# The second products of the last expert stage in a fixed TensorE order, with their weights laid out by halves

## The chip, the cores and the metric

The kernel runs on one core of a Trainium2 chip, in one launch. The number that counts is the device time of the launch in microseconds (us), the median over several executions. A core has five engines that run their own instruction streams side by side and wait for each other by semaphores: TensorE (PE; its weight loads are shown apart as PEld), VectorE (DVE), ScalarE (ACT), GpSimd (POOL) and SyncE (SP), which here issues almost all transfers. Sixteen DMA engines move the data.

## The reference

The program computes a stack of layers; the change lies in the second of two layers of routed experts. Each of 16 experts picks its 64 tokens of 512, multiplies them by its weights, and the weighted results are added back at the places of those tokens:

```python
def moe_ec(h, router_w, w1, w3, w2):
    cap = EC_CAPACITY * T // N_EXPERTS          # 2 * 512 // 16 = 64
    ...
    gate, idx = lax.top_k(jnp.swapaxes(aff, 1, 2), cap)
    xg = h[bidx, idx]
    a = jnp.einsum('becd,edf->becf', xg, w1)
    g = jnp.einsum('becd,edf->becf', xg, w3)
    y = jnp.einsum('becf,efd->becd', jax.nn.silu(a) * g, w2)
    y = y * gate[..., None].astype(y.dtype)
    return jnp.zeros_like(h).at[bidx, idx].add(y.astype(h.dtype))
```

All three weights of an expert are 1024 x 1024 in f32. "Up products" are those with w1 and w3, "second products" those with w2. What comes behind is a second kind of block, which begins with a norm and one large projection, `w_in`.

## The kernel before

The kernel has five stages, ssd, moe0, attn, moe1 and ffn. In moe1 (`moe_last`) the experts are taken in eight pairs; the two experts of a pair stand side by side in TensorE's columns (`tile_position` 0 and 64). First all eight pairs do their up products (`moe_up`), and their results `aT` are kept. Then the second products follow by halves of the 1024 output features: all eight pairs for features 0 to 511, and again for features 512 to 1023. One pair in one half is called a unit here; there are 16, numbered 0 to 15. In a unit (`moe_down` with `half` set):

- the product: 16 matmuls `py<-...,aT` (L1348), eight steps k of the contraction for each of two experts. Its weights are four tiles of 1 MB from the ring (below).
- ACT scales the product by the gate into `yhi` (L1354), DVE makes the remainder `ylo` (L1355), so that hi plus lo carry f32 through the faster format.
- the slots matmul `sp` (L1361) and DVE's compare `ohT` (L1365): a 0/1 matrix that says which token each row belongs to.
- the scatter: for each of four feature tiles j, two matmuls `sc` (hi L1372, lo L1373), and DVE adds the result into the residual stream `xT` (L1374).

`sc` and `sp` take their PSUM tiles under tag "x", which the table in `Banks` sends to name D, two banks; `py` lies in name A.

The ring (`Ring`, L106 to 133) hands out weight tiles in turn: two from the pool `wm` (one transfer of 1 MB each), then three made of two `raw` buffers each (two transfers of 512 KB); there are six raw buffers, and other loads use them too. A transfer waits on SP until its buffer is free, and SP issues in order. A new ring is made for each half.

Behind the first half, `hd.feed(k)` for k = 0 to 3 starts the norm of the next block on the four finished feature tiles of `xT` (DVE and ACT write `stk`, the normed input, and sums of squares; POOL adds some). `hd.begin` then computes, tile by tile, the first four contraction steps of 12 tiles of `w_in`: each of these head tiles is 12 matmuls (`mm<-stk,hwh/hwl`, L475 to L477), with weights split into `hwh` by ACT (L176) and `hwl` by POOL (L177). Six of the 12 are handed out between the units of the second half, the other six come behind it. The later steps (k = 4 to 7, `mm<-stk,whi`) need the second half's features.

The order in which each engine sees this is made by a scheduler that weighs which instruction could go next; only inside `manual_schedule` does an engine take them in the order of the program. On the stretch of the change no such block stands before.

Of the kernel before, what the change touches and what calls it, by code (L numbers as in the profile page):

```python
# [379 lines left out]
class Kern:  # L380
# [835 lines left out]
    def moe_last(self, st, R, head):  # L1216
# [19 lines left out]
        for pr in range(8):  # L1236
            after = self.after(R[0], pr, pp)
            if pr < 8 - DEFER:
                self.moe_down(layer, pr, R, ring, ep, pp, self.moe_up(layer, pr, R, ring, ep, pp, after))
            else:  # L1240
                acts.append(self.moe_up(layer, pr, R, ring, ep, pp, after, ap))
# [81 lines left out]

    def moe_down(self, layer, pr, R, ring, ep, pp, acts, half=None):

        nc = self.nc
        big, small = R[0], (R[1] if len(R) > 1 else None)
        sel, iop = self.mk["sel"], self.mk["iop"]
        aT, cT = acts

        def bank(nm, tag, bufs):
            return pp.tile([P, 512], F32, name=nm, tag=tag, bufs=bufs)

        yb = lambda k, e: aT[:, k, 64 * e:64 * e + 64]
        ys = (lambda k, e: cT[:, k % 4, 64 * e + 32 * (k // 4):64 * e + 32 * (k // 4) + 32]) if small else None
        if half is None:
            py = [bank("py", "a", 2) for _ in range(2)]
            cy = bank("cy", "c", 2) if small else None
            self.moe_product(layer, "moe_w2", pr, ring, yb, ys, py, cy)
        else:  # L1340
            py = [None, None]
            py[half] = bank("py", "a", 2)
            for q in range(2):
                w = [ring.tile(self.I["moe_w2"][layer, 2 * pr + e, q * 512:(q + 1) * 512, half * 512:(half + 1) * 512], 4) for e in range(2)]
                for a in range(4):
                    k = 4 * q + a
                    for e in range(2):
                        nc.tensor.matmul(py[half][64 * e:64 * e + 64, :], yb(k, e), w[e][a], start=(k == 0), stop=(k == KT - 1), tile_position=(0, 64 * e))  # L1348


        def scaled(src, gate):
            hi = ep.tile([P, 512], F32R, name="yhi", tag="yhi", bufs=2)
            lo = ep.tile([P, 512], F32R, name="ylo", tag="ylo", bufs=2)
            nc.scalar.activation(hi, src, AF.Copy, scale=gate)  # L1354
            nc.vector.scalar_tensor_tensor(lo, src, gate, hi.bitcast(F32), op0=ALU.mult, op1=ALU.subtract)  # L1355
            return hi, lo

        def slots(s, cols):
            n = s.n
            ps = bank("sp", "x", 2)  # L1360
            nc.tensor.matmul(ps[:, 0:n], sel[:, pr].rearrange("p e j -> p (e j)"), s.slotT, start=True, stop=True)  # L1361
            r = []
            for cix in cols:
                t = ep.tile([P, 512], F32R, name="ohT", tag="ohT", bufs=2)
                nc.vector.tensor_scalar(t[:, 0:n], ps[:, 0:n], iop[:, cix:cix + 1], None, op0=ALU.is_equal)  # L1365
                r.append(t[:, 0:n])
            return r

        def scatter(s, y, o, k, kk):
            n, c, res = s.n, s.c, s.res  # L1370
            ps = bank("sc", "x", 2)
            nc.tensor.matmul(ps[:, 0:n], y[0][:, kk * P:(kk + 1) * P], o, start=True, stop=False)  # L1372
            nc.tensor.matmul(ps[:, 0:n], y[1][:, kk * P:(kk + 1) * P], o, start=False, stop=True)  # L1373
            nc.vector.scalar_tensor_tensor(res[:, k, :], ps[:, 0:n], self.mod(layer, 5, c, k), res[:, k, :], op0=ALU.mult, op1=ALU.add)  # L1374

        ob = slots(big, (0,))[0]
        for hf in (range(2) if half is None else (half,)):
            y = scaled(py[hf], big.gate[:, pr:pr + 1])
            for j in range(4):
                scatter(big, y, ob, hf * 4 + j, j)  # L1380
        if small:
            y = scaled(cy, small.gate[:, pr:pr + 1])
            for hf, o in enumerate(slots(small, (1, 2))):
                for j in range(4):
# [1096 lines left out]
```

## Time and profile before

| | us |
|---|---|
| median of 3 executions | 3331.31 (3325.92 to 3332.93) |
| the profiled execution | 3335.19 |
| its span in the trace | 3333.5 |
| product 0 of the stage scaled (yhi starts) | 2230.05 |
| product 7, the last of the first half | 2312.68 |
| product 8, the first of the second half | 2329.70 |
| product 15, the last | 2424.3 |
| first late matmul of the next block | 2447.55 |

The times of instructions count from the span's start and come from one profiled execution. In a timeline row the first number is the start, the second the length, and what stands in brackets is the engine's idle time before it and what ended it. Several instructions of one kind in a row are one line with a count. In the second half the trace shows each `py` matmul as records of its own, and a few records can be missing. The share of busy time over the whole span says little about this stretch, since the stages have different limits; the windows show it alone.

### The profile page before, as it was taken

To read this page: it belongs to the slowest core of one execution; us is meant where nothing else is said; L and a number is where in the kernel's file an instruction comes from. 1 tells how busy PE (TensorE), PEld (TensorE's weight loads), DVE (VectorE), ACT (ScalarE), POOL (GpSimd) and SP (SyncE) were. 2 spreads that over 40 slices of the span, in tenths; PEclk is the share of its full clock that TensorE was granted. 3 is DMA by queue.
4 is the path that set the end of the run, shared out by engine and by line. 5 is a ranking of instruction groups with operands and counts; after the bars stand their busy time and mean duration, and the time that the engine had idled before them with its cause. 6 is when DMAs were issued, how large, how long until landed. Compare 5 with 4: busy or idle time off the path is not lost.

```text
span 3333.5 us, 47840 instructions
## 1 busy us (share of the span) xinstructions
PE 3143.5 (94%) x18944; PEld 2061.6 (62%) x18944; DVE 1644.7 (49%) x3014; ACT 1165.3 (35%) x2063; POOL 963.3 (29%) x694
## 2 busy tenths in 40 slices
PE   7999999889999999999999899988999999999998
PEld 4677777777744343435757644422467778988886
DVE  5588888987521121114466410014369864763312
ACT  4344444455511111114566410001155353673222
POOL 1344555544200000002501200000054443145543
PEclk9999999999999999999999899999999999999999
DMA  7355433354388989893261599999932224443332
GB/s 251 120 168 162 143 89 93 99 168 161 124 314 318 369 323 365 322 370 131 65 215 39 215 368 409 409 389 332 339 119 75 76 69 144 134 159 105 95 92 85
DMA packets 254096, 668.60 MB, mean 201 GB/s; under 512 B 19312, under 2 KB 73456, under 8 KB 252848
## 3 DMA queue, kind: packets, MB, share of 16 engines
q1 hardware_dynamic: 243920, 645.42, 54.1%
q10 hardware_dynamic: 9952, 20.12, 1.8%
q8 instruction: 149, 2.44, 0.3%
q14 instruction: 75, 0.61, 0.1%
HBM read 651.65 MB, written 13.83 MB: 200 GB/s over the span
## 4 chain that ended last, share of the span: by engine, by line
PE 60%; DVE 9%; DMA 4%; ACT 2%; issue 2%; POOL 1%; SPq 0%; DVEq 0%; ACTq 0%; POOLq 0%
PE mm L475 6%; PE mm L477 6%; PE mm L476 6%; PE py L1348 4%; PE py L1102 3%; PE pg L1102 3%; PE pa L1102 3%; PE pa L1270 3%; DMA wm<-in_moe_w_dram 3%; PE pg L1270 2%; PE gth L343 2%; PE cy L1104 2%; PE cg L1104 2%; PE ca L1104 2%; PE pv L1564 1%
## 5 line engine op out<-in xcount | busy, mean ns | idle before, releaser
L446 POOL TENSOR_TENSOR wlo<-raw,whi 128x1024 fp32r<-128x1024 f32 (+3 forms) x207 | 460.8, 2228 | 639.1 <-ACT whi L445 605.6
L445 ACT CAST whi<-raw 128x1024 fp32r<-128x1024 f32 (+2 forms) x291 | 285.9, 984 | 478.0 <-PE mm L476 204.9
L475 PE MATMUL mm<-stk,whi 128*128 128x512 f32 (+2 forms) x944 | 342.8, 363 | 0.3 <-DVE pt__23886 L1709 0.3
L477 PE MATMUL mm<-stk,wlo 128*128 128x512 f32 (+2 forms) x944 | 336.2, 356 | 0.0
L476 PE MATMUL mm<-stk,whi 128*128 128x512 f32 (+2 forms) x944 | 335.0, 355 | 0.0
L475 PE MATMUL pin<-hhi,whi 128*128 128x256 f32 (+1 forms) x768 | 272.2, 355 | 5.3 <-DVE acc L813 3.8
L477 PE MATMUL pin<-hhi,wlo 128*128 128x256 f32 (+1 forms) x768 | 266.3, 347 | 0.0
L476 PE MATMUL pin<-hlo,whi 128*128 128x256 f32 (+1 forms) x768 | 263.9, 344 | 0.0
L475 PEld LDWEIGHTS mm<-stk,whi 128*128 128x128 f32 (+1 forms) x944 | 179.9, 191 | 33.3 <-issue 7.9
L58 POOL TENSOR_TENSOR sqa<-sqa,sq 128x256 f32<-128x256 f32 (+1 forms) x56 | 64.6, 1154 | 467.7 <-DVE acc L204 409.9
L476 PEld LDWEIGHTS mm<-stk,whi 128*128 128x128 f32 (+1 forms) x944 | 179.8, 190 | 30.1 <-issue 6.1
L1166 POOL TENSOR_TENSOR cT<-cT,scc 128x256 f32<-128x256 f32 x56 | 39.6, 736 | 545.4 <-ACT scc L1165 544.9
L477 PEld LDWEIGHTS mm<-stk,wlo 128*128 128x128 f32 (+1 forms) x944 | 179.2, 190 | 25.9 <-issue 1.1
L475 PEld LDWEIGHTS pin<-hhi,whi 128*128 128x128 f32 x768 | 147.0, 192 | 46.9 <-issue 20.9
L1188 DVE TENSOR_TENSOR ac<-ac,pg 128x512 f32<-128x512 f32 x16 | 11.0, 687 | 301.3 <-PE pg L1102 301.3
L476 PEld LDWEIGHTS pin<-hlo,whi 128*128 128x128 f32 x768 | 147.2, 192 | 19.9 <-DVE hlo L602 2.7
L477 PEld LDWEIGHTS pin<-hhi,wlo 128*128 128x128 f32 x768 | 147.1, 192 | 18.5 <-issue 1.7
L813 DVE SCALAR_TENSOR_TENSOR acc<-pin,cwh,acc 128x511 f32<-128x511 f32 (+3 forms) x256 | 148.5, 607 | 15.1 <-ACT acc L808 13.5
L1302 DVE TENSOR_TENSOR ac<-ac,pg 128x512 f32<-128x512 f32 x16 | 11.0, 685 | 249.7 <-PE pg L1270 249.7
L867 DVE SCALAR_TENSOR_TENSOR m<-ab,acum,m 128x128 f32<-128x128 f32 x192 | 121.3, 675 | 22.1 <-POOL m L865 22.1
L446 DVE TENSOR_TENSOR wlo<-raw,whi 128x1024 fp32r<-128x1024 f32 (+1 forms) x84 | 105.4, 1258 | 40.6 <-ACT whi L445 37.0
L872 POOL TENSOR_TENSOR ce<-ce,xc 128x1024 f32<-128x1024 f32 (+1 forms) x48 | 103.4, 2155 | 39.6 <-ACT ce L871 39.5
(716 smaller groups left out, 7179.3 us busy)
## 6 DMA issues: line engine op xcount, KB each, us to landing
wm<-in_moe_w_dram SPq DMA_DIRECT2D x255, 1024.0 KB, 9.5
raw<-in_moe_w_dram SPq DMA_DIRECT2D x258, 512.0 KB, 9.0
raw<-in_ada_w_dram SPq DMA_DIRECT2D x96, 512.0 KB, 4.7
raw<-in_w_f_dram SPq DMA_DIRECT2D x68, 512.0 KB, 3.7
raw<-in_w_ssd_in_dram SPq DMA_DIRECT2D x48, 512.0 KB, 4.5
ab<-aS SPq DMA_DIRECT2D x96, 256.0 KB, 4.7
raw<-in_w_in_dram SPq DMA_DIRECT2D x33, 512.0 KB, 3.7
raw<-in_w_ssd_out_dram SPq DMA_DIRECT2D x32, 512.0 KB, 3.8
```

The source lines that it names most:

```text
L445: nc.scalar.copy(hi[:, 0:n], raw[:, 0:n])
L446: (eng or self.lo).tensor_tensor(lo[:, 0:n], raw[:, 0:n], hi[:, 0:n].bitcast(F32), op=ALU.subtract)
L475: nc.tensor.matmul(ps, wh, ah, start=start, stop=False)
L476: nc.tensor.matmul(ps, wh, al, start=False, stop=False)
L477: nc.tensor.matmul(ps, wl, ah, start=False, stop=stop)
L813: nc.vector.scalar_tensor_tensor(o, p_[:, lo + s:hi + s], tap(j), o, op0=ALU.mult, op1=ALU.add)
L867: nc.vector.scalar_tensor_tensor(m[:, r, :], ab[:, r, :], acum[:, c, 4 * g + r:4 * g + r + 1], m[:, r, :], op0=ALU.subtract, op1=ALU.min)
L872: nc.gpsimd.tensor_tensor(ce[:, j0:j1, :], ce[:, j0:j1, :], conv["C"][:, o:o + P].unsqueeze(1).to_broadcast([P, j1 - j0, P]), op=ALU.mult)
L1102: nc.tensor.matmul(pb[z][o:o + 32, :], lb(k, e)[:, 32 * h:32 * h + 32], w[e][k % 2][:, z * 512:(z + 1) * 512], tile_position=(0, o), **f)
L1104: nc.tensor.matmul(pc[o:o + 32, :], ls(k, e), w[e][k % 2][:, h * 512:(h + 1) * 512], tile_position=(0, o), **f)
L1270: nc.tensor.matmul(pb[hf][64 * e:64 * e + 64, :], lb(k, e), w[e][a][:, hf * 512:(hf + 1) * 512], tile_position=(0, 64 * e), **f)
L1348: nc.tensor.matmul(py[half][64 * e:64 * e + 64, :], yb(k, e), w[e][a], start=(k == 0), stop=(k == KT - 1), tile_position=(0, 64 * e))
```

## The change

The second products get a function of their own, `moe_halves`, and `moe_down` goes. Four things differ:

- PE's order is that of the program: product of unit u, scatter of unit u-1, slots of the next unit, and from unit 9 on one head tile. Seven head tiles stand in front of the last scatter, five behind it.
- the scatter outputs take tags "x" and "c" in turn, so names D and B with two banks each; the slots matmul stays on D.
- one ring runs over all 16 units.
- w2 of the second layer is laid out on the host as [half, expert, partition, step k, 512]. A partition of a wm tile is then one run of 8 KB and that of a raw buffer one of 4 KB, with 16 KB from one partition to the next; before it was four, or two, runs of 2 KB.

```diff
-        v = src.rearrange("(a p) n -> p a n", p=P)
+        v = src if len(src.shape) == 3 else src.rearrange("(a p) n -> p a n", p=P)
...
-        for hf in range(2):
-            ring = Ring(self, self.wm1[:1], 3)
-            for i in range(DEFER):
-                self.moe_down(layer, 8 - DEFER + i, R, ring, ep, pp, acts[i], hf)
-                for _ in range(HEAD * (i + 1) // (2 * DEFER) - HEAD * i // (2 * DEFER)):
...
+        self.moe_halves(layer, R[0], ep, pp, acts, hd)
+        return hd
+
+    def moe_halves(self, layer, big, ep, pp, acts, hd):
...
+        ring = Ring(self, self.wm1[:1], 3)
...
+        def product(pr, half):
+            py, aT = bank("py", "a"), acts[pr][0]
+            for q in range(2):
+                w = [ring.tile(self.I["moe_w2h"][half, 2 * pr + e, :, 4 * q:4 * q + 4, :], 4) for e in range(2)]
...
+        def scatter(y, o, half):
+            for j in range(4):
+                k = 4 * half + j
+                ps = bank("sc", "xc"[j % 2])
+                for z in range(2):
+                    nc.tensor.matmul(ps, y[z][:, j * P:(j + 1) * P], o, start=(z == 0), stop=(z == 1))
+                nc.vector.scalar_tensor_tensor(big.res[:, k, :], ps, self.mod(layer, 5, 0, k), big.res[:, k, :], op0=ALU.mult, op1=ALU.add)
+
         fill = iter(())
+        with self.tc.manual_schedule(engines={mybir.EngineType.PE}):
+            last, o = None, slots(0)
+            for u in range(16):
+                half, pr = divmod(u, 8)
+                y = product(pr, half)
+                if last:
+                    scatter(*last)
+                last = (y, o, half)
+                if u < 15:
+                    o = slots((u + 1) % 8)
+                if u == 8:
+                    for k in range(4):
+                        hd.feed(k)
+                    fill = hd.begin(ep, pp)
+                elif u > 8:
+                    next(fill, None)
+            scatter(*last)
         for _ in fill:
             pass
...
+    A["moe_w2h"] = i["moe_w2"][1].reshape(NE, KT, P, 2, 512).transpose(3, 0, 2, 1, 4)
```

Outside moe1's second products the order of instructions is the same on every engine. Where it moves, on PE in the first half, before (`py` product, `sc` scatter outputs, `sp` slots):

```order
L1372 MATMUL sc<-ohT,yhi 128x512 x2
L1373 MATMUL sc<-ohT,ylo 128x512 x2
L1372 MATMUL sc<-ohT,yhi 128x512
L1373 MATMUL sc<-ohT,ylo 128x512
L1348 MATMUL py<-raw,aT 64x512 x2
L1372 MATMUL sc<-ohT,yhi 128x512
L1373 MATMUL sc<-ohT,ylo 128x512
L1348 MATMUL py<-raw,aT 64x512 x5
L1361 LDWEIGHTS sel
L1361 MATMUL sp<-xslotT,sel 128x512
```

and now:

```order
L1266 MATMUL py<-raw,aT 64x512 x8
L1266 MATMUL py<-wm,aT 64x512 x8
L1279 MATMUL sc<-ohT,yhi 128x512
L1279 MATMUL sc<-ohT,ylo 128x512
L1279 MATMUL sc<-ohT,yhi 128x512
L1279 MATMUL sc<-ohT,ylo 128x512
L1279 MATMUL sc<-ohT,yhi 128x512
L1279 MATMUL sc<-ohT,ylo 128x512
L1279 MATMUL sc<-ohT,yhi 128x512
L1279 MATMUL sc<-ohT,ylo 128x512
L1254 LDWEIGHTS sel
L1254 MATMUL sp<-xslotT,sel 128x512
```

Before, the scatter of a unit began right behind its product, and part of it stood inside the next product; now the scatter behind a product is that of the unit before, with hi and lo of one output together, and the slots matmul behind it.

On PE in the second half (`mm<-stk,hwh` and `hwl` are the head tiles), before:

```order
L475 MATMUL mm<-stk,hwh 128x512
L1372 MATMUL sc<-ohT,yhi 128x512 x2
L476 MATMUL mm<-stk,hwh 128x512
L1373 MATMUL sc<-ohT,ylo 128x512 x2
L477 MATMUL mm<-stk,hwl 128x512
L475 MATMUL mm<-stk,hwh 128x512
L476 MATMUL mm<-stk,hwh 128x512
L477 MATMUL mm<-stk,hwl 128x512
L1372 MATMUL sc<-ohT,yhi 128x512
L1373 MATMUL sc<-ohT,ylo 128x512
L475 MATMUL mm<-stk,hwh 128x512
```

and now, one head tile (nine of its twelve matmuls are between the two pieces):

```order
L1279 MATMUL sc<-ohT,yhi 128x512
L1279 MATMUL sc<-ohT,ylo 128x512
L1254 LDWEIGHTS sel
L1254 MATMUL sp<-xslotT,sel 128x512
L475 MATMUL mm<-stk,hwh 128x512
L476 MATMUL mm<-stk,hwh 128x512
L477 MATMUL mm<-stk,hwl 128x512
L1266 MATMUL py<-wm,aT 64x512 x8
L1266 MATMUL py<-raw,aT 64x512 x8
L1279 MATMUL sc<-ohT,yhi 128x512
```

Before, head matmuls and scatter matmuls mixed; now a whole head tile stands between slots and the next product.

On DVE where the first half ends (`xT<-sc` scatter adds, `stk` and `acc` the feeds, `ohT` the compare behind the slots matmul), before:

```order
L1374 SCALAR_TENSOR_TENSOR xT<-sc,mods_81,xT 128x512 x4
L199 SCALAR_TENSOR_TENSOR stk<-xT,gg,stk 128x512
L204 TENSOR_SCALAR acc_18078<-sqa,fin_18050 128x512
L199 SCALAR_TENSOR_TENSOR stk<-xT,gg,stk 128x512
L206 SCALAR_TENSOR_TENSOR acc_18078<-sq,fin_18050,acc_18078 128x512
L199 SCALAR_TENSOR_TENSOR stk<-xT,gg,stk 128x512
L206 SCALAR_TENSOR_TENSOR acc_18078<-sq,fin_18050,acc_18078 128x512
L1365 TENSOR_SCALAR ohT<-sp,iop 128x512
L1355 SCALAR_TENSOR_TENSOR ylo<-py,xgate,yhi 128x512
L1374 SCALAR_TENSOR_TENSOR xT<-sc,mods_81,xT 128x512 x4
```

and now:

```order
L1271 SCALAR_TENSOR_TENSOR ylo<-py,xgate,yhi 128x512
L1280 SCALAR_TENSOR_TENSOR xT<-sc,mods_81,xT 128x512 x3
L1256 TENSOR_SCALAR ohT<-sp,iop 128x512
L199 SCALAR_TENSOR_TENSOR stk<-xT,gg,stk 128x512
L204 TENSOR_SCALAR acc_18078<-sqa,fin_18050 128x512
L199 SCALAR_TENSOR_TENSOR stk<-xT,gg,stk 128x512
L206 SCALAR_TENSOR_TENSOR acc_18078<-sq,fin_18050,acc_18078 128x512
L199 SCALAR_TENSOR_TENSOR stk<-xT,gg,stk 128x512
L206 SCALAR_TENSOR_TENSOR acc_18078<-sq,fin_18050,acc_18078 128x512
L1280 SCALAR_TENSOR_TENSOR xT<-sc,mods_81,xT 128x512
L1271 SCALAR_TENSOR_TENSOR ylo<-py,xgate,yhi 128x512
L1280 SCALAR_TENSOR_TENSOR xT<-sc,mods_81,xT 128x512 x3
```

In both, the feeds stand in one piece. Before, they followed the last adds of the first half and stood in front of `ohT` of unit 8; now `ohT` of unit 9 is in front of them, and the first add of unit 8's scatter behind them.

## Rows read from the trace of the kernel before

**Rows 1.** The page: span, and busy time of PE.

```profile
span 3333.5 us, 47840 instructions
...
PE 3143.5 (94%) x18944; PEld 2061.6 (62%) x18944; DVE 1644.7 (49%) x3014; ACT 1165.3 (35%) x2063; POOL 963.3 (29%) x694
```

**Rows 2.** Busy time by windows: first half, switch, second half, tail.

```profile
core 0: us, PE busy (x) PEld busy (x) DVE busy (x) ACT busy (x) POOL busy (x), PEclk, DMA share, GB/s
2230.00:2312.68 82.68, 74.51 (x287) 24.05 (x285) 30.33 (x42) 4.81 (x7) 0.00 (x0) 1.00 0.97 355
2312.68:2329.70 17.02, 14.29 (x43) 4.12 (x43) 12.30 (x14) 5.44 (x9) 4.75 (x3) 0.80 0.77 275
2329.70:2424.30 94.60, 91.36 (x358) 38.33 (x359) 30.30 (x42) 12.89 (x22) 10.10 (x8) 1.00 0.92 331
2424.30:2447.55 23.25, 20.70 (x80) 15.98 (x81) 17.79 (x15) 13.38 (x22) 13.64 (x12) 0.93 0.54 195
```

**Rows 3.** DMA totals: 2060 to 2200 (up products), then 2235 to 2252.

```profile
DMA packets 15057, 57.26 MB, mean 409 GB/s; under 512 B 1094, under 2 KB 1094, under 8 KB 15051
...
DMA packets 3375, 6.57 MB, mean 386 GB/s; under 512 B 171, under 2 KB 171, under 8 KB 3374
```

**Rows 4.** ACT's scaling line L1354: instances, and what ended its idle time.

```profile
L1354 ACT ACTIVATE yhi<-py,xgate x16: 687/687/689, 2230.0 to 2424.3; 128x512 fp32r<-128x512 f32 x16
...
  PE py L1348: 126.5, 16
```

**Rows 5.** Timeline of PE, one unit of the first half (start, length, engine, line).

```profile
2291.72 0.50 PE L1372 MATMUL sc<-ohT,yhi 128*128 128x512 f32 x1 [0.61 <-DVE xT L1374]
...
2293.29 0.37 PE L1361 MATMUL sp<-xslotT,sel 16*128 16x512 bf16 x1 [0.18 <-DVE xT L1374]
2293.60 0.64 PE L1348 MATMUL py<-wm,aT 128*64 128x512 f32 x1
...
2295.36 0.59 PE L1348 MATMUL py<-wm,aT 128*64 128x512 f32 x1
...
2295.79 0.59 PE L1348 MATMUL py<-wm,aT 128*64 128x512 f32 x1
...
2301.45 0.73 PE L1372 MATMUL sc<-ohT,yhi 128*128 128x512 f32 x2 [0.77 <-ACT yhi L1354]
```

**Rows 6.** Timeline at the half switch, PE's, then SP's.

```profile
2317.84 1.84 PE L1348 MATMUL py<-wm,aT 128*64 128x512 f32 x2 [0.34 <-DMA wm<-in_moe_w_dram]
2320.45 5.35 PE L1348 MATMUL py<-wm,aT 128*64 128x512 f32 x13 [0.78 <-DMA wm<-in_moe_w_dram]
...
2312.63 0.92 SPq L125 DMA_DIRECT2D wm<-in_moe_w_dram  x2
```

**Rows 7.** Timeline of PE in the second half, scatter and head matmuls.

```profile
2344.01 0.39 PE L1372 MATMUL sc<-ohT,yhi 128*128 128x512 f32 x1
2344.24 0.40 PE L1373 MATMUL sc<-ohT,ylo 128*128 128x512 f32 x1
2344.47 0.40 PE L475 MATMUL mm<-stk,hwh 128*128 128x512 f32 x1
```

**Rows 8.** Timeline of DVE at the half switch: adds, feeds, ohT.

```profile
2316.32 1.41 DVE L1374 SCALAR_TENSOR_TENSOR xT<-sc,mods,xT 128x512 f32<-128x512 f32 x2 [0.17 <-PE sc L1373]
2317.66 0.74 DVE L199 SCALAR_TENSOR_TENSOR stk<-xT,gg,stk 128x512 fp32r<-128x512 f32 x1
...
2319.37 1.75 DVE L206 SCALAR_TENSOR_TENSOR acc<-sq,fin,acc 128x512 f32<-128x512 f32 x1
...
2325.72 0.74 DVE L1365 TENSOR_SCALAR ohT<-sp,iop 128x512 fp32r<-128x512 f32 x1
```

**Rows 9.** Timeline of PE in the tail, up to the first late matmul.

```profile
2435.70 0.50 PE L477 MATMUL mm<-stk,hwl 128*128 128x512 f32 x1 [0.55 <-POOL hwl L177]
...
2440.77 0.77 PE L477 MATMUL mm<-stk,hwl 128*128 128x512 f32 x1 [2.00 <-POOL hwl L177]
...
2447.55 0.39 PE L475 MATMUL mm<-stk,whi 128*128 128x512 f32 x1
```

More of the change, by code (lines that the diff above doesn't have):

```diff
@@ L1224, in moe_last @@
         sx = ExitStack()
-        ring = Ring(self, self.wm1[:-1], 3, [(self.pool(sx, "moe_wx", bufs=DEFER // 2), DEFER // 2)])
+        ring = Ring(self, self.wm1[:-1], 3, [(self.pool(sx, "moe_wx", bufs=4), 4)])
         place = []
@@ L1236, in moe_last @@
         for pr in range(8):
[L1237 to L1241, printed above, removed]
+            acts.append(self.moe_up(layer, pr, R, ring, ep, pp, self.after(R[0], pr, pp), ap))
         wa.close()
@@ L1244, in moe_last, with slots @@
         hd = head()
-        fill = iter(())
-        for hf in range(2):
-            ring = Ring(self, self.wm1[:1], 3)
-            for i in range(DEFER):
-                self.moe_down(layer, 8 - DEFER + i, R, ring, ep, pp, acts[i], hf)
-                for _ in range(HEAD * (i + 1) // (2 * DEFER) - HEAD * i // (2 * DEFER)):
+        self.moe_halves(layer, R[0], ep, pp, acts, hd)
+        return hd
+    def moe_halves(self, layer, big, ep, pp, acts, hd):
+        nc = self.nc
+        sel, iop = self.mk["sel"], self.mk["iop"]
+        ring = Ring(self, self.wm1[:1], 3)
+        bank = lambda nm, tag: pp.tile([P, 512], F32, name=nm, tag=tag, bufs=2)
+        def slots(pr):
+            ps = bank("sp", "x")
+            nc.tensor.matmul(ps, sel[:, pr].rearrange("p e j -> p (e j)"), big.slotT, start=True, stop=True)
+            t = ep.tile([P, 512], F32R, name="ohT", tag="ohT", bufs=2)
+            nc.vector.tensor_scalar(t, ps, iop[:, 0:1], None, op0=ALU.is_equal)
+            return t
+        def product(pr, half):
+            py, aT = bank("py", "a"), acts[pr][0]
+            for q in range(2):
+                w = [ring.tile(self.I["moe_w2h"][half, 2 * pr + e, :, 4 * q:4 * q + 4, :], 4) for e in range(2)]
+                for a in range(4):
+                    k = 4 * q + a
+                    for e in range(2):
+                        nc.tensor.matmul(py[64 * e:64 * e + 64, :], aT[:, k, 64 * e:64 * e + 64], w[e][a], start=(k == 0), stop=(k == KT - 1), tile_position=(0, 64 * e))
+            hi = ep.tile([P, 512], F32R, name="yhi", tag="yhi", bufs=2)
+            lo = ep.tile([P, 512], F32R, name="ylo", tag="ylo", bufs=2)
+            gate = big.gate[:, pr:pr + 1]
+            nc.scalar.activation(hi, py, AF.Copy, scale=gate)
+            nc.vector.scalar_tensor_tensor(lo, py, gate, hi.bitcast(F32), op0=ALU.mult, op1=ALU.subtract)
+            return hi, lo
+        def scatter(y, o, half):
[5 more added lines that the diff above has]
+                nc.vector.scalar_tensor_tensor(big.res[:, k, :], ps, self.mod(layer, 5, 0, k), big.res[:, k, :], op0=ALU.mult, op1=ALU.add)
+        fill = iter(())
+        with self.tc.manual_schedule(engines={mybir.EngineType.PE}):
[13 more added lines that the diff above has]
+                elif u > 8:
@@ L1322, in moe_up @@
         return aT, cT
[L1324 to L1384, printed above, removed]
-                    scatter(small, y, o, hf * 4 + j, j)
@@ L2315 @@
 APART = 3
-DEFER = 8
 STAGES = ["ssd", "moe0", "attn", "moe1", "ffn"]
@@ L2440, in prepare @@
     A["w_ao"] = wtiles(w)
-    for n in ("moe_w1", "moe_w3", "moe_w2"):
+    for n in ("moe_w1", "moe_w3"):
         A[n] = i[n]
+    A["moe_w2"] = i["moe_w2"][0:1]
+    A["moe_w2h"] = i["moe_w2"][1].reshape(NE, KT, P, 2, 512).transpose(3, 0, 2, 1, 4)
     w = i["w_in_2"][0]
```

7 lines of the change are left out of this document (1 added, 6 removed).

## The prediction

> **What bounds the kernel now.** I read the page first: TensorE (PE) is busy for 94% of the span [rows 1], so only a place where PE waits, or where its work itself shrinks, can give time. The change touches one stretch, the second products of the last expert stage, from the first scaling of a product (yhi at 2230.05) to the first late matmul of the block behind it (2447.55). The table of windows cuts this stretch into first half, switch, second half and tail [rows 2]. In it PE works 74.51 of 82.68 us, then 14.29 of 17.02, 91.36 of 94.60, and 20.70 of 23.25: 16.7 us without work, and 217.55 us in all. A unit (one pair of experts, one half of the features) brings 4.19 MB of weights. The spacing of the first eight units is 82.68/7 = 11.81 us, in which 355 GB/s arrive.
>
> Next, who waits. ScalarE (ACT) scales each product and is idle for 126.5 us over 16 times "until PE py" [rows 4], so ACT is no limit; PE in turn waits for ACT. The timeline of one unit shows the round [rows 5]: product, 0.77 us idle until yhi is there, two scatter outputs, 0.61 us until VectorE (DVE) has emptied a bank (the xT add), 0.18 us more in front of the slots matmul. That is a chain of PE, ACT and DVE, one after the other. The product itself starts a matmul every 0.43 us (2295.36 to 2295.79): 16 x 0.4275 = 6.84 us.
>
> Is the DMA a limit beside it? With 4 KB runs of weights (the up products before, 2060 to 2200) the queue carries 409 GB/s; with the 2 KB runs of the second products, at their start where it is filled, 386 [rows 3]. At these rates a unit takes 10.25 and 10.86 us. So the chain (11.81) stands little above the transfers, and once it is gone the transfers decide.
>
> **The change part by part.** *One unit behind.* PE's order is now product(u), scatter(u-1), slots(u+1). yhi and ylo of a unit have a whole product in which to be made, so the 0.77 goes. Scatter outputs lie alternately in D and B, four banks, so outputs 3 and 4 don't wait for adds 1 and 2, and the 0.61 goes. Without waits a scatter matmul follows the last in 0.233 us [rows 7]: 8 x 0.233 = 1.87. With the slots matmul (0.31, [rows 5]) PE needs 6.84 + 1.87 + 0.31 = 9.0 us for a unit of the first half, below 10.25: the first half becomes bound by the weights.
>
> *Layout.* The loads become 8 KB (wm) and 4 KB (raw) of one run per partition instead of 2 KB. No row here shows 8 KB weights, so the nearest rows bound it: 386 (no effect) to 409 (as the 4 KB runs). I take 409, the row with runs of the kind that the raw loads will have. Lower than 386 is rival 3.
>
> *One ring over both halves.* Before, the second half makes a new ring, whose first two loads go into the buffers used last: SyncE (SP) issues them at 2312.63, after product 7, and PE waits 0.34 and 0.78 us for them while the granted clock is 0.80 over the switch [rows 2, 6]. Now tile i is issued when tile i-5 is free, without a break at unit 8. When a pair of tiles starts to be used, three more (3.1 MB, 7.7 us of transfer) are still to come, and the pair frees its buffers within 3.4 us, so the queue does not run dry.
>
> Sum of the first half: product 0 ended at 2230.05 - 0.6 (its yhi starts some 0.6 behind the last matmul's start). Its 4.19 MB at 409 instead of 386 come 0.6 us sooner, but part of them is loaded earlier; I put its end at 2229.4. Units 1 to 8 at 10.25 give 82.0: product 8 ends at 2311.4, where it ended shortly before 2329.70. Gain so far 18 us.
>
> *Unit 9 and the feeds.* Behind scatter(7) the stage gives four feeds to DVE (stk and acc), which in the trace took from 2317.66 to 2325.72, 8.06 us, with single instructions drawn out to 1.75 where GpSimd (POOL) worked beside them [rows 8]. In the new DVE order they stand before the xT add of scatter(8). From the end of product 8 (T8) DVE has add, ylo, three adds and ohT (0.65 + some 4.1 at 0.67 to 0.75 each, ready at T8 + 4.8), the feeds (to 12.9), and the add of scatter(8) output 0 (to 13.6). The slots matmul of unit 10 reuses that bank. PE gets there at T8 + 10.25 + 1.87 = 12.1, and waits until about 13.8: 1.7 us. This is an added wait; queued behind it on PE are the first head tile and product(10), and all that follows waits too. Bounds: 0 (feeds without POOL beside them, 5.6) to 4.5 (2.9, and 1.6 for a lowered clock behind it as in the tail, (1 - 0.93) x 23.25 [rows 2]). I take 1.7. Then slots 0.31, head tile 12 x 0.233 = 2.79, product 6.84: product 10 ends at T8 + 13.8 + 9.94 + 0.3 = T8 + 24.0 = 2335.4.
>
> *Units 11 to 15.* PE now does a head tile in every unit (seven of the twelve, before six): 6.84 + 1.87 + 0.31 + 2.79 + 0.3 for the changes between kinds (before, PE was busy 91.36 for 8 x 9.02 + 6 x 2.79 = 88.9) = 12.1. The transfers need 10.25 and 0.64 for half a pair of head weights: 10.9, below 12.1, so PE decides. Five units: 60.5, product 15 ends at 2395.9. Before, it ended at about 2424.3: gain 28. The second half before shows what this rests on: 94.60 us with 91.36 of work, 11.83 a unit with six tiles in it; here seven tiles over seven units cost more a unit, and fewer are left for the tail. Head weights share six raw buffers with the ring, so a ring load six places on waits until POOL has made both hwl. In the new ACT and POOL order these casts come early enough (before yhi(9) and yhi(13), behind yhi(11), with more than 5 us to spare). I cost it at nothing; if that cover went, 2 to 3 us in each of three places.
>
> *Tail.* scatter(14) 1.87, tile seven 2.79, scatter(15) 1.87, five tiles 13.95, 0.4 between: 20.9, to 2416.8. In the tail before, PE waited 0.55 and 2.00 for hwl from POOL, and the granted clock over the tail was 0.93, which costs (1 - 0.93) x 23.25 = 1.6 [rows 2, 9]. POOL still has the same instructions in almost the same order, so I keep 4 us of these 4.2 (bounds 0 to 6): the first late matmul at 2420.8, against 2447.55. DVE's last feeds (8 to 11 us) lie beside the five tiles as before.
>
> Sum: 2447.55 - 2420.8 = 26.75 us. What follows is the same on every engine, and PE waits for nothing at 2447.55, so I carry it to the end in full. The profiled execution took 3335.19: 3308.4. The median is 3.88 below that execution: 3304.6, so 3305.
>
> **A rule against the layout.** The trace has 386 GB/s with 2 KB runs and 409 with 4 KB runs [rows 3]. The Trainium skill ("DMA: Bandwidth & Descriptors", Specifications) says that transfers of 512 B or more already go at line rate; by that rule the layout gives nothing, which is rival 1. The same table puts the HBM limit of a core near 358 GB/s; by that a unit would take 11.7 us, an estimate from that page, and about 12 us of the gain would go. The 409 of this trace speaks against the second figure here, and the step from 386 to 409 against the first.
>
> **Rivals.** *1. The rate stays at 386.* The two rates differ in more than the run length (the up products have more buffers in flight). Then units 0 to 9 take 0.61 us more each, 6 us: gain 20.7, 3311. For it: the rows don't separate the two causes. Against: the 386 stands where the DMA share is full, too. 14%.
>
> *2. The fixed order makes PE wait at every head tile.* Before, PE's order let sc and head matmuls mix; now PE stands at a tile until its hwl is there, with a product behind it. If each of the seven tiles in the loop cost what the worst one in the tail cost, 2.0 + 1.6, that is 25 us: gain 2, 3330. Against: in the loop POOL does nothing but hwl, 1.3 us each, and the weights come a unit ahead. 12%.
>
> *3. Slower: the weights land more slowly than before.* Partitions now step by 16 KB in HBM, and each transfer is 128 such runs. If the rate fell under 193.2/15 = 12.9 us a unit, that is 326 GB/s, the transfers would be the bound of all 16 units, and the kernel slower. At 300 GB/s, 14.0 us: 15 x 14.0 + 24.9 from 2229.4 ends at 2464, 17 us later, 3348. For it: no row has this step. Against: every full queue in [rows 3] runs at 386 or more. 5%.
>
> *The change doesn't do what it says*, so that PE would still wait for yhi: the order on PE excludes it.
>
> **How the numbers follow.** My forecast has 69%: 3305, on its own 3296 to 3314 (the wait at unit 10 by 1.7 less or 2.8 more, the tail by 4 less or 2 more, the rate between the two rows). Rival 1 lies inside; the range goes to 3293 and 3323, and leaves out most of rivals 2 and 3 and a little below: about 2 in 10. A difference under 0.2% (6.7 us) can't be told from none. Faster by more: forecast, rival 1 and a quarter of rival 2, 86%; within: over half of rival 2, 7%; slower: rival 3 and the rest, 7%.
>
> **What would show it.** Right: yhi every 10.2 to 10.4 us in the first half with 400 GB/s or more; no wait for a wm load and full clock around unit 8; a wait of PE for xT in front of one slots matmul, 1 to 3 us; 12.1 us a unit behind it; sc never waiting for yhi; the late matmul 27 us sooner. Wrong: yhi at 10.9 (rival 1), PE idle until hwl or a DMA at the head tiles (rival 2), or units of 13 us with the DMA full (rival 3).

## The result: 0.5% faster, within the range, by two thirds of the predicted gain

| | before | changed |
|---|---|---|
| median, us | 3330.67 (4 runs, 3325.92 to 3332.93) | 3312.69 (4 runs, 3311.26 to 3315.73) |
| the profiled execution, us | 3335.19 | 3311.26 |
| its span in the trace, us | 3333.5 | 3309.5 |

The ratio is 0.9950, with a 95% interval of 0.9937 to 0.9964: 18.0 us of the median, where 26.75 were predicted. Measured once more, beside two other kernels, the changed kernel had 3308.92 against 3325.87, a ratio of 0.9946 (0.9929 to 0.9963).

The two profiled executions differ by 24 us, and not all of that is the change. The first yhi of the stage came at 2223.71 instead of 2230.05, and 4.2 of these 6.3 us stand already at the first scaled product of the first expert layer (1008.9 against 1013.1), which is the same in both. In the eleven runs of the experiments below the start of the stage lies anywhere between 2216.5 and 2228.4. So I compare the stretch from the first yhi to the first late matmul, which holds all that the change moves. It took 217.50 us before [rows 2, 9] and 200.84 after: 16.7 us. A second profile of the changed kernel gave 199.77, so differences of a microsecond in it mean nothing.

The page of the changed kernel, the busy times of [rows 1]:

```profile
PE 3129.0 (95%) x18944; PEld 2070.5 (63%) x18944; DVE 1638.5 (50%) x3014; ACT 1165.6 (35%) x2063; POOL 965.6 (29%) x694
```

The windows of the changed kernel: product 0 to 8, 8 to 10, 10 to 15, each from yhi to yhi, and the tail; the last row is a piece of the second, which is used below.

```profile
core 0: us, PE busy (x) PEld busy (x) DVE busy (x) ACT busy (x) POOL busy (x), PEclk, DMA share, GB/s
2223.71:2307.62 83.91, 79.55 (x321) 32.11 (x320) 29.71 (x44) 5.51 (x8) 0.00 (x0) 1.00 1.02 409
2307.62:2335.68 28.06, 23.92 (x95) 11.05 (x96) 18.13 (x20) 7.76 (x13) 8.15 (x5) 0.88 0.79 299
2335.68:2401.09 65.41, 63.99 (x266) 30.76 (x267) 20.21 (x30) 9.36 (x16) 5.07 (x4) 1.00 0.86 328
2401.09:2424.55 23.46, 21.48 (x89) 16.18 (x89) 17.93 (x19) 13.51 (x23) 15.73 (x13) 1.00 0.65 235
2323.20:2328.00 4.80, 4.80 (x12) 3.40 (x12) 3.21 (x5) 0.00 (x0) 0.00 (x0) 0.52 1.02 416
```

Against [rows 2]: the first half runs with a full queue at 409 GB/s, at the full clock into unit 8 and beyond; the switch has gone as a stretch of its own. But the second window has 4.1 us without work and a clock of 0.88, and the third has 1.4 us without work. What PE waited for in the whole stretch (us in total, times, longest), before:

```profile
PE sc L1372 <- ACT yhi L1354: 7.7, 10, 0.8
PE sc L1372 <- DVE xT L1374: 3.7, 6, 0.6
```

and now:

```profile
PE py L1266 <- DMA wm<-in_moe_w2h_dram: 4.8, 4, 1.8
PE sp L1254 <- DVE xT L1280: 4.1, 1, 4.1
PE mm L477 <- POOL hwl L177: 1.7, 2, 1.1
PE py L1266 <- DMA raw<-in_moe_w2h_dram: 0.8, 1, 0.8
```

No wait for yhi is left, and none of a scatter for an add. The wait for xT stands in one place, and it is the longest of all:

```profile
2318.63 0.40 PE L1279 MATMUL sc<-ohT,ylo 128*128 128x512 f32 x1
2323.17 0.58 PE L1254 MATMUL sp<-xslotT,sel 16*128 16x512 bf16 x1 [4.14 <-DVE xT L1280]
...
2324.27 0.63 PE L476 MATMUL mm<-stk,hwh 128*128 128x512 f32 x1
2324.70 0.63 PE L477 MATMUL mm<-stk,hwl 128*128 128x512 f32 x1
```

The scatter of unit 8 ends, the slots matmul of unit 10 stands for 4.14 us, and the head tile behind it runs with matmuls 0.43 apart instead of 0.23, until 2327.7. From 2323.2 to 2328 the granted clock is 0.52 (the last of the windows above), the lower level of 1.2 instead of 2.4 GHz; ahead of the idle stretch it was 1.00. What slots waited for on DVE:

```profile
2312.24 0.74 DVE L199 SCALAR_TENSOR_TENSOR stk<-xT,gg,stk 128x512 fp32r<-128x512 f32 x1
...
2313.96 1.77 DVE L206 SCALAR_TENSOR_TENSOR acc<-sq,fin,acc 128x512 f32<-128x512 f32 x1
...
2320.71 1.74 DVE L206 SCALAR_TENSOR_TENSOR acc<-sq,fin,acc 128x512 f32<-128x512 f32 x1
2322.38 0.74 DVE L1280 SCALAR_TENSOR_TENSOR xT<-sc,mods,xT 128x512 f32<-128x512 f32 x1
```

And what worked beside it on POOL:

```profile
2313.60 4.97 POOL L58 TENSOR_TENSOR sqa<-sqa,sq 128x512 f32<-128x512 f32 x3 [408.47 <-PE py L1266]
2318.53 3.38 POOL L177 TENSOR_TENSOR hwl<-raw,hwh 128x512 fp32r<-128x512 f32 x2
```

The reader should see here that the feeds took 10.1 us (2312.24 to 2322.38) and not the 8.06 of [rows 8]: five of the eight instructions are drawn out to 1.74 to 1.78, three beside POOL's three sqa adds, as before, and two more beside two hwl.

The pace of the units, by the start of yhi (units 7 to 14 here):

```profile
2297.49 0.69 ACT L1270 ACTIVATE yhi<-py,xgate 128x512 fp32r<-128x512 f32 x1 [11.50 <-PE py L1266]
2307.62 0.69 ACT L1270 ACTIVATE yhi<-py,xgate 128x512 fp32r<-128x512 f32 x1 [9.44 <-PE py L1266]
...
2317.39 0.68 ACT L1270 ACTIVATE yhi<-py,xgate 128x512 fp32r<-128x512 f32 x1
...
2335.68 0.69 ACT L1270 ACTIVATE yhi<-py,xgate 128x512 fp32r<-128x512 f32 x1 [6.47 <-PE py L1266]
...
2348.05 0.69 ACT L1270 ACTIVATE yhi<-py,xgate 128x512 fp32r<-128x512 f32 x1 [4.28 <-PE py L1266]
...
2362.07 0.69 ACT L1270 ACTIVATE yhi<-py,xgate 128x512 fp32r<-128x512 f32 x1 [8.14 <-PE py L1266]
...
2374.49 0.69 ACT L1270 ACTIVATE yhi<-py,xgate 128x512 fp32r<-128x512 f32 x1 [1.13 <-PE py L1266]
...
2388.68 0.69 ACT L1270 ACTIVATE yhi<-py,xgate 128x512 fp32r<-128x512 f32 x1 [8.28 <-PE py L1266]
```

The first half has eight units in 83.9 us (10.49 each). From unit 10 on units of 12.4 alternate with units of 14.0 and 14.2.

Waits are the smaller part of what went. The whole stretch, before and now, and one unit without a wait in each (unit 3 before, unit 4 now), columns as above:

```profile
2230.05:2447.55 217.50, 200.81 (x766) 82.47 (x766) 90.72 (x113) 36.52 (x59) 28.49 (x22) 0.98 0.89 321
2223.71:2424.55 200.84, 188.93 (x768) 90.09 (x767) 85.98 (x113) 36.14 (x59) 28.95 (x22) 0.98 0.89 347
...
2253.87:2265.27 11.40, 11.32 (x43) 3.23 (x41) 4.41 (x6) 0.69 (x2) 0.00 (x0) 1.00 1.04 380
2255.75:2265.16 9.41, 9.41 (x42) 3.76 (x43) 4.04 (x6) 0.69 (x1) 0.00 (x0) 1.00 1.00 389
```

PE's time without work fell from 16.7 to 11.9 us, its busy time from 200.8 to 188.9 at the same mean clock. So 11.9 of the 16.7 us are the same matmuls standing closer together: before, the scatter of a unit stood in pieces inside the next product, and such a unit took 11.4 us with PE at work throughout, where 9.4 do now. e9 below puts 5 us of this on the order alone; what the rest comes from wasn't taken apart.

### The profile page after: what moved, and what is told of

Its sections match the earlier page's. It is cut to its first block, busy times and chain, and to the rows that moved or that the text cites. A ratio compares the mean times of both kernels' runs of the same rounds, so it can differ in the third digit from the quotient of the medians.

```text
span 3309.5 us, 47859 instructions
## 1 busy us (share of the span) xinstructions
PE 3129.0 (95%) x18944; PEld 2070.5 (63%) x18944; DVE 1638.5 (50%) x3014; ACT 1165.6 (35%) x2063; POOL 965.6 (29%) x694
## 4 chain that ended last, share of the span: by engine, by line
PE 60%; DVE 8%; DMA 5%; ACT 2%; issue 2%; POOL 1%; SPq 0%; DVEq 0%; ACTq 0%; POOLq 0%
PE mm L475 7%; PE mm L476 7%; PE mm L477 7%; PE py L1102 3%; PE pg L1102 3%; PE pa L1102 3%; PE pa L1313 3%; PE py L1266 3%; PE pg L1313 2%; DMA wm<-in_moe_w_dram 2%; PE gth L343 2%; PE cy L1104 2%; PE cg L1104 2%; PE ca L1104 2%; DMA raw<-in_moe_w_dram 1%
## 5 line engine op out<-in xcount | busy, mean ns | idle before, releaser
L445 ACT CAST whi<-raw 128x1024 fp32r<-128x1024 f32 (+2 forms) x291 | 285.7, 984 | 477.7 <-PE mm L476 200.8
```

What stands on the lines that cost most here:

```text
L445: nc.scalar.copy(hi[:, 0:n], raw[:, 0:n])
```

## The experiments

All stretches are from the first yhi to the first late matmul, in us, of one profile for each kernel (the second profile of the changed kernel, e10, is 1.1 us shorter than the first, so a cost read against it is that much larger and a saving that much smaller); the columns behind it are its parts from yhi to yhi. Medians stand beside runs of the kernel before on the same chip, shared by the kernels that were measured together (e1 to e4, e5 to e8, e9 to e11).

| kernel | median | before beside it | ratio (95%) | stretch | units 0 to 8 | 8 to 10 | 10 to 15 | tail |
|---|---|---|---|---|---|---|---|---|
| before (profile) | | | | 217.5 | 99.6 | 27.8 | 66.8 | 23.3 |
| changed | 3312.69 | 3330.67 | 0.9950 (0.9937 to 0.9964) | 200.8 | 83.9 | 28.1 | 65.4 | 23.5 |
| e1 old layout | 3318.26 | 3326.60 | 0.9967 (0.9955 to 0.9980) | 206.4 | 88.1 | 27.5 | 67.3 | 23.5 |
| e2 before, new layout | 3328.79 | 3326.60 | 1.0001 (0.9989 to 1.0013) | 216.6 | 98.8 | 27.8 | 66.8 | 23.3 |
| e3 ring per half | 3314.22 | 3326.60 | 0.9966 (0.9954 to 0.9979) | 207.2 | 89.5 | 29.0 | 64.3 | 24.4 |
| e4 slots on C | 3307.37 | 3326.60 | 0.9934 (0.9918 to 0.9951) | 195.1 | 84.3 | 22.9 | 64.5 | 23.5 |
| e5 scatter on D only | 3320.67 | 3325.65 | 0.9990 (0.9981 to 1.0000) | 213.7 | 88.9 | 30.8 | 69.4 | 24.6 |
| e6 scatter at once | 3319.57 | 3325.65 | 0.9977 (0.9968 to 0.9986) | 210.0 | 88.0 | 27.9 | 70.4 | 23.8 |
| e7 head weights apart | 3308.98 | 3325.65 | 0.9943 (0.9928 to 0.9958) | 197.5 | 84.4 | 27.9 | 61.8 | 23.5 |
| e8 e4 and e7 together | 3298.39 | 3325.65 | 0.9918 (0.9905 to 0.9931) | 191.5 | 83.7 | 22.4 | 61.9 | 23.5 |
| e9 scheduler's order | 3311.12 | 3325.87 | 0.9951 (0.9936 to 0.9966) | 203.7 | 86.9 | 25.6 | 67.3 | 23.9 |
| e10 changed, again | 3308.92 | 3325.87 | 0.9946 (0.9929 to 0.9963) | 199.8 | 84.8 | 27.6 | 64.0 | 23.4 |
| e11 e8, again | 3301.46 | 3325.87 | 0.9922 (0.9902 to 0.9942) | 192.1 | 84.4 | 22.4 | 61.9 | 23.4 |

**e1, the old layout of the weights in the changed kernel.**

```diff
-                w = [ring.tile(self.I["moe_w2h"][half, 2 * pr + e, :, 4 * q:4 * q + 4, :], 4) for e in range(2)]
+                w = [ring.tile(self.I["moe_w2"][1, 2 * pr + e, q * 512:(q + 1) * 512, half * 512:(half + 1) * 512], 4) for e in range(2)]
...
```

> The changed kernel with w2 as it lay before, in runs of 2 KB. Measured from the first yhi to the first late matmul (before 217.5 us, changed kernel 200.8). Theory, the run length sets the rate of the full queue: the first half falls from 409 to about 386 GB/s, its eight units take 86 to 88 us instead of 83.9, and the second half waits some more for loads; the stretch is 204 to 208 us, so 3 to 7 us of the 17 come from the layout. Rival, the rate comes from the queue being kept full and not from the runs: 400 GB/s or more and the stretch within 1.5 us of 200.8.

Its first half, busy times and rate as in the windows above:

```profile
2225.52:2313.62 88.10, 81.31 (x321) 30.55 (x321) 29.71 (x44) 5.51 (x9) 0.00 (x0) 1.00 1.05 385
```

385 GB/s with a DMA share of 1.05, against 409 with 1.02 (400 with 1.01 in the second profile, e10): same kernel, same ring, only the layout differs. The theory holds, with 88.1 for 86 to 88 predicted and a stretch of 206.4. The layout is worth 5.5 us. The edit changes the steps between the runs along with their length, so it doesn't part the two; for the length speaks that the up products, whose weights lie as before in runs of 4 KB, have 409 as well [rows 3]. The Trainium skill ("DMA: Bandwidth & Descriptors", Specifications) would have 2 KB at line rate like anything from 512 B; the 385 and 409 here say that for this load it is not.

**e2, the layout alone, in the kernel before.** The line of e1 the other way round, in `moe_down`, with the weights laid out to match.

> The kernel before with the new layout of w2 alone. Theory, its first half is bound by the chain product, yhi, scatter, add (11.8 us a unit) and not by the weights: first half 82 to 83 us as before (82.6), the stretch 214 to 218, and the same time within 0.1%. Rival, the weights bind already there: first half 78 us or less and the kernel 5 us or more faster.

The stretch is 216.6, the ratio 1.0001: nothing. Up to unit 6 the units take the same 11.4 to 12.2 us as before; units 7 and 8 together take 28.1 instead of 29.0. Together with e1 this says that the layout pays only once the old order has gone: the same edit is worth nothing before the rest of the change and 5.5 us after it.

**e3, a new ring for the second half.**

```diff
-        ring = Ring(self, self.wm1[:1], 3)
+        rings = [Ring(self, self.wm1[:1], 3)]
...
         def product(pr, half):
+            if half == 1 and pr == 0:
+                rings.append(Ring(self, self.wm1[:1], 3))
+            ring = rings[-1]
             py, aT = bank("py", "a"), acts[pr][0]
```

> The changed kernel with a new ring for the second half, as before the change. Theory: the first loads of unit 8 wait for product 7, PE waits for them and its clock is lowered, the stretch grows by 4 to 8 us to 205 to 209. Rival, scatter and slots cover the loads: within 1.5 us of 200.8.

```profile
2304.82 1.04 PE L1269 MATMUL py<-wm,aT 128*64 128x512 f32 x2 [2.04 <-DMA wm<-in_moe_w2h_dram]
2307.20 4.92 PE L1269 MATMUL py<-wm,aT 128*64 128x512 f32 x13 [1.34 <-DMA wm<-in_moe_w2h_dram]
```

PE waits 2.04 and 1.34 us for the loads of unit 8; its yhi comes 15.5 us behind that of unit 7 instead of 10.1. The stretch is 207.2: the theory holds, one ring is worth some 6 us. The median (3314.22) shows less of it than the stretch, and the two ratios' intervals overlap.

**e4, the slots matmul on name C.**

```diff
         def slots(pr):
-            ps = bank("sp", "x")
+            ps = bank("sp", "g")
```

> The changed kernel with the slots matmul in PSUM name C instead of D, where it shares banks with scatter output 0. Theory: the wait of 4.1 us at unit 10 for the xT add behind the feeds goes, and with it the lowered clock of the first head tile (4.8 instead of 2.8 us): the stretch shrinks by 5 to 6.5 us to 194 to 196. Rival, the feeds delay something else on PE there (the next scatter, or the head tile waits for stk or hwl) or the ring has not filled up by then: less than 3 us.

```profile
2322.12 0.40 PE L1279 MATMUL sc<-ohT,ylo 128*128 128x512 f32 x1
2322.45 0.39 PE L1254 MATMUL sp<-xslotT,sel 16*128 16x512 bf16 x1
...
2324.15 0.40 PE L475 MATMUL mm<-stk,hwh 128*128 128x512 f32 x1
2324.38 0.40 PE L476 MATMUL mm<-stk,hwh 128*128 128x512 f32 x1
```

The place of the 4.14 us: slots follows the scatter at once, and behind a wait of 0.31 for the first hwl the head matmuls are 0.23 apart again. Units 8 to 10 take 22.9 instead of 28.1 (and 27.6 in the second profile), the stretch 195.1. The theory holds: the bank shared with scatter output 0 was all that tied slots to the feeds, and the wait with its slow clock cost 5 us. The feeds themselves are as long as in the changed kernel; no slots matmul waits for them now.

**e5, all scatter outputs on D.**

```diff
-                ps = bank("sc", "xc"[j % 2])
+                ps = bank("sc", "x")
```

> The changed kernel with all scatter outputs in PSUM name D again (two banks, shared with slots). Stretch from the first yhi to the first late matmul: changed kernel 200.8 us. Theory: scatter outputs 3 and 4 and the slots matmul wait for xT adds, about 1 us a unit; in the first half the weights (10.25 us a unit) hide it, y0 to y8 stays within 2 us of 83.9; from unit 10 on, where PE sets the pace, it costs 0.6 to 1.4 a unit, so the stretch is 205 to 210. Rival, the banks are needed in the first half as well: units of 11 us or more there.

```profile
2264.99 0.40 PE L1279 MATMUL sc<-ohT,ylo 128*128 128x512 f32 x1
2265.76 0.50 PE L1279 MATMUL sc<-ohT,yhi 128*128 128x512 f32 x1 [0.38 <-DVE xT L1280]
...
2267.08 0.50 PE L1279 MATMUL sc<-ohT,yhi 128*128 128x512 f32 x1 [0.58 <-DVE xT L1280]
```

Outputs 3 and 4 wait 0.38 and 0.58 for the adds; with the wider gaps between the matmuls around these waits it is 1.5 us a unit from unit 10 on (13.9 instead of 12.4). In the first half the theory fails and the rival is nearer: 10.9 us a unit, five of the eight, and 88.9 us where at most 85.9 were expected. I had 9.0 + 1 there, hidden by 10.25; without a wait PE needs 9.4 (the unit shown above), and with these 10.9. The new layout's rate isn't used then (385 GB/s). The stretch, 213.7, lies beyond the 205 to 210 of the theory. Without the four banks the rest of the change keeps 0.1% of the time, at the edge of none (ratio 0.9990, up to 1.0000).

**e6, each unit's scatter behind its own product.**

```diff
-            last, o = None, slots(0)
+            o = slots(0)
...
                 y = product(pr, half)
-                if last:
-                    scatter(*last)
-                last = (y, o, half)
+                scatter(y, o, half)
...
-            scatter(*last)
```

> The changed kernel with each unit's scatter directly behind its own product instead of one unit behind; four banks, fixed order, layout and ring as in the change. Theory: PE waits about 0.8 us for yhi in each unit (and for ylo); in the first half the weights hide it (9.0 + 0.8 is below 10.25), in the second half it costs about 0.8 for each of eight units: stretch 205 to 209. Rival, the chain again sets the pace everywhere: 11.5 us or more a unit in the first half, stretch 215 or more.

```profile
2268.63 0.49 PE L1279 MATMUL sc<-ohT,yhi 128*128 128x512 f32 x1 [0.81 <-ACT yhi L1270]
2269.42 0.50 PE L1279 MATMUL sc<-ohT,ylo 128*128 128x512 f32 x1 [0.29 <-DVE ylo L1271]
```

Two waits a unit, 0.81 for yhi and 0.29 for ylo, and a unit takes 10.8 in the first half (PE's 9.4, 1.1 of waits, and wider gaps behind them), 13.8 from unit 10 on. So the weights don't hide the waits in the first half, as the theory had it. The stretch is 210.0, one above the theory's range and well under the rival's 215. The feeds cost less here: the scatter of unit 8 waits 2.2 us for its ylo behind them (the next yhi comes 14.1 later). It is the waits in each unit that add up.

**e7, the head weights in a buffer of their own.** The first seven tiles are loaded one at a time into 2 KB of their own per partition; the last five stay in the raw buffers.

```diff
-        for j in range(0, len(self.tiles), 2):
-            ms = self.tiles[j:j + 2]
-            raw = K.rw.tile([P, 1024], F32, name="raw", tag="raw")
+        own = [[m] for m in self.tiles[:7]]
+        rest = self.tiles[7:]
+        for i, ms in enumerate(own + [rest[j:j + 2] for j in range(0, len(rest), 2)]):
+            raw = wp.tile([P, n], F32, name="hraw", tag="hraw", bufs=1) if i < 7 else K.rw.tile([P, 1024], F32, name="raw", tag="raw")
```

> The changed kernel with the weights of the first seven head tiles loaded into a buffer of their own, one tile at a time, instead of into the six raw buffers that the ring uses. Theory: the dips of the transfers in the second half and PE's waits for loads in units 12 and 14 (14.0 and 14.2 us instead of 12.4) come from the head loads' turn in these buffers; without it units 11 to 15 take 12.4 each, and the stretch is 196.5 to 198.5. Rival, the ring of five tiles is too short for 12.1 us of PE work a unit whoever shares it: no change (200 or more).

```profile
2328.76:2390.59 61.83, 61.83 (x266) 29.50 (x267) 20.22 (x30) 9.45 (x15) 5.08 (x4) 1.00 0.93 352
```

In this third window PE now has no idle time at all, and every unit takes 12.35 to 12.38. The theory holds. What the shared buffers did in the changed kernel, on SP:

```profile
2335.64 0.81 SPq L171 DMA_DIRECT2D raw<-in_w_in_dram  x2
2336.54 10.09 SPq L130 DMA_DIRECT2D raw<-in_moe_w2h_dram  x4
2346.68 2.33 SPq L125 DMA_DIRECT2D wm<-in_moe_w2h_dram  x2
...
2361.22 0.33 SPq L125 DMA_DIRECT2D wm<-in_moe_w2h_dram  x1
2369.29 0.81 SPq L171 DMA_DIRECT2D raw<-in_w_in_dram  x2
```

And on PE, for the longer units 12 and 14:

```profile
2356.72 1.02 PE L1266 MATMUL py<-wm,aT 128*64 128x512 f32 x2
2358.38 3.65 PE L1266 MATMUL py<-wm,aT 128*64 128x512 f32 x14 [0.64 <-DMA wm<-in_moe_w2h_dram]
...
2385.00 3.65 PE L1266 MATMUL py<-raw,aT 128*64 128x512 f32 x14 [0.78 <-DMA raw<-in_moe_w2h_dram]
```

The load of two head tiles at 2335.64 takes one turn in the six raw buffers, so each ring load behind it gets its buffer half a tile later. Four raw loads take 10.09 us to issue, the two wm loads behind them in SP's order go out at 2346.68, and PE waits in the middle of product 12. The next such load (2369.29) stands in front of a wm load: between 2361.55 and 2369.29 SP issues nothing, since it waits for product 13 to free the head load's raw buffer:

```profile
SPq L171 <- PE py L1266: 7.7, 1, 7.7
```

The DMA share falls to 0.65 over this stretch, and product 14 waits. The profile puts 0.64 and 0.78 on the loads, but the units are 1.65 and 1.8 longer (0.6 and 1.5 in e10); the rest stands in wider gaps around these waits, which the profile puts on nothing. SP also waited twice 1.1 us until POOL's hwl had freed a buffer. e7 takes away the turn and this hold together and so doesn't part them; by SP's waits the turn is the larger.

**e8, e4 and e7 together.**

> Both together: slots on C (stretch 195.1 us alone) and the head weights in a buffer of their own. Theory: the two costs are separate, the stretch is 191 to 193.5 and the time 8 to 10 us below the changed kernel. Rival, without the wait at unit 10 the transfers are what is late, and the stretch stays at 194 or more.

The stretch is 191.5: both costs go, and they add (5.7 and 3.3 alone, 9.3 together; against e10 each is 1.1 less). The kernel is the fastest of all, 0.9918 of before (0.9905 to 0.9931), against 0.9950 (0.9937 to 0.9964) of the changed kernel.

**e9, the scheduler's order.**

```diff
-        with self.tc.manual_schedule(engines={mybir.EngineType.PE}):
+        if True:
```

> The changed kernel without the fixed order: the scheduler again decides the order on PE, with the program, the banks, the ring and the layout of the change. It puts the first units' scatters right behind their own products, later ones inside the next product, and mixes head matmuls with products. Theory, one unit behind is what takes yhi and the adds off PE's path, and the scheduler keeps it in part: first half as in the change (84 to 86 us, the weights decide), the rest 2 to 6 us longer than with the fixed order, stretch 203 to 207. Rival, the scheduler's mixing fills the waits (the one of 4.1 us at unit 10 above all) better than the fixed order: stretch below 200.

```profile
2217.82:2421.51 203.69, 194.01 (x766) 83.63 (x766) 85.46 (x112) 36.39 (x59) 27.97 (x22) 1.00 0.88 342
```

The stretch is 203.7, in the theory's range (the first half, 86.9, is 0.9 above what it had), with waits for yhi back (4.9 us in all), but none at unit 10: units 8 to 10 take 25.6. The waits are not what it loses by: PE stands still for 9.7 us in all, less than the 11.9 of the fixed order, but is busy for 194.0 instead of 188.9, as in the mixed units before. The fixed order is worth 3 to 4 us of the stretch; in the median it can't be told from none (0.9951 against 0.9946 beside it).

**e10 and e11, the changed kernel and e8 side by side.**

> The changed kernel once more, beside the two others of this call on the same chip: stretch 200 to 202 us, the time about 0.5% below the kernel before.

> Slots on C and the head weights in a buffer of their own, once more beside the changed kernel on the same chip. Theory: stretch 191 to 192.5 and 8 to 10 us below the changed kernel in time. Rival, part of this was the chip of the other call: less than 6 us.

The stretches are 199.8 (200 to 202 expected) and 192.1, the medians 3308.92 and 3301.46: 7.5 us, and 7.6 by the stretch. That is a little below the 8 to 10 expected, above the rival's 6. The two ratios' intervals overlap here; the stretches are far apart.

## Why the prediction came out as it did

The range held the time, and the direction and the main steps were right; the gain was put at 26.75 and is 18.0, so the forecast of 3305 was 8 us low. By the prediction's own steps, from the first yhi:

| step | predicted | measured |
|---|---|---|
| units 1 to 8 | 82.0 | 83.9 |
| units 9 and 10 | 24.0 | 28.1 |
| units 11 to 15 | 60.5 | 65.4 |
| tail, from yhi of unit 15 | 24.3 | 23.5 |
| sum | 190.8 | 200.8 |

- *One unit behind, four banks: right.* No scatter waits. e6 and e5 put 9 and 13 us on them; each is needed. But the waits were the smaller part of what stood above the weights' 10.25: of the 11.81 us a unit they make 1.2, and PE was busy for 10.6 (74.51 us over seven units), not for 9.0. The prediction doesn't ask why. And 9.0 was short by 0.4: a unit without a wait takes 9.4 in the new order, too. Where the weights decide this cost nothing; it is why e5 and e6 came out longer in the first half than I had them.
- *Weights at 409: right.* The rate of the first half is 409 to the number (400 in e10), and e1 shows that it comes with the layout, so rival 1 is out. The units are not even: 9.4 to 12.2 us, longest where PE waits for a wm load (units 2 and 7, 11.35 and 12.19). The 1.9 us beyond 82.0 are transfer, too: 83.91 us at 409 GB/s carry 34.3 MB, 0.8 MB more than eight units need, so the loads were further ahead at the end of the first half than at its start.
- *One ring: right*, 6 us by e3.
- *The wait at unit 10: right in kind and place, wrong in size.* The step "the feeds (to 12.9)" took them at 8.06 us from the old trace. There POOL did three sqa adds beside them; now it does two hwl as well, and two more feeds are drawn out, so 10.1. They also began 0.4 later than I had it. PE came to the slots matmul when I had it, 12.0 behind the end of product 8 for 12.1 (product 9 came 0.5 sooner, the scatter took longer), and so the wait was 4.14 instead of 1.7. And I left out of the value, though not out of its bounds, that the clock was lower behind the wait: the head tile took 4.8 instead of 2.8. The two add 4.4 us, of which 4.1 show in units 9 and 10. Wait and clock together were 6.1, beyond the upper bound of 4.5.
- *Units 11 to 15: the step that failed.* "I cost it at nothing; if that cover went, 2 to 3 us in each of three places": it went in two, at 1.65 and 1.8. I had looked at when a buffer held by a head load comes free again, with more than 5 us to spare; it was not quite in time (1.1 us twice). I had not looked at the turn that the load takes: it shifts every ring load behind it by half a tile, and SP issues in order, so that a head load that waits (7.7 us) holds up the ring's loads. e7 removes both, and the units go from 13.1 on average to 12.37. The rest, 0.27 a unit, is the 12.1 of the sum, which was that much short.
- *Tail: right within a microsecond.* The waits for hwl were 1.7 instead of 2.6, and the clock did not fall.
- The remaining difference between 16.7 us of the stretch and 18.0 of the medians is less than the spread of the runs.

With the two costs undone (e8) the stretch is 191.5, where the prediction had 190.8 with a wait of 1.7 in it. That is the check on the rest of the sum: without that wait it was 2.4 us short, 1.7 in the first half and 1.4 in units 11 to 15, less 0.8 in the tail.

Of the signs named beforehand, the rate, the full clock without a wait for a load around unit 8, the scatter that never waits and the wait in front of one slots matmul came as said, that wait longer than the 1 to 3 us. The units were not as even as 10.2 to 10.4 and 12.1, and the late matmul came 23 us sooner, 6.3 of them from the earlier start.

## What to carry to other kernels

Before counting waits, look at how densely the engine works between them: here 11.9 of the 16.7 us were busy time, about 5 of them by the order alone (e9). When a chain of waits goes, the next limit stands close behind it: work out the transfers' own time for each unit first, and expect edits that were worth nothing before (the layout here, e2) to be worth something after (e1). A load that joins a ring of buffers costs its turn, not only the time for which it holds one; and a wait on a bank is often a wait for everything that stands in front of the reader on its engine, so that another bank (e4, one tag) is cheaper than making that work faster.

## What the runs showed of the hardware

- The rate of a full queue changed with the layout of the weights: 385 to 386 GB/s with runs of 2 KB (e1, [rows 3]), 409 with runs of 4 KB [rows 3], and 400 to 409 with a mix of 8 and 4 KB in steps of 16 KB (first halves of the changed kernel, e4, e7, e8, e10 and e11). Length and step of the runs were not varied apart.
- DVE instructions with two inputs in SBUF go from 0.74 to 1.74 to 1.78 us while POOL works, and POOL's hwl from 1.27 to 1.69 beside them, while adds with one input from PSUM keep their 0.67 to 0.75 (three from 2350.00 on beside an hwl of 2349.33 to 2350.62). The Trainium skill ("SBUF — State Buffer", "SBUF: two separate sides") calls the port pair of the two engines an exclusive lock held for a whole instruction; the drawn-out feeds, one for each of POOL's five instructions, agree with it.
- A stop of PE of 4.14 us was followed by 4.5 us at a granted clock near the lower level (0.52); the stop cost half as much again as it lasted. Of shorter stops, one and the same wait for a load in unit 1, 1.76 to 1.79 us, left the clock at 1.00 over the unit in five profiles (changed kernel, e1, e3, e4, e8; 10.5 to 10.8 us) and was followed by the lower clock in two, e7 and e11 (0.86 over the unit, 11.8 and 11.9 us):

```profile
2216.53:2228.34 11.81, 10.02 (x34) 2.85 (x33) 1.41 (x2) 0.68 (x1) 0.00 (x0) 0.86 1.02 413
```

- In the changed kernel the waits of units 2 and 7 (0.91 and 1.44 us) and of units 12 and 14 (0.64 and 0.78) left the clock at 1.00 over their windows.
